# A four-layer decoder trunk: the instruction order drawn with the scheduler's time-line simulation

## The chip, the core and the metric

The kernel runs on one core of a Trainium2 chip. A core has TensorE (PE, matrix products; PEld is its weight load), VectorE (DVE), ScalarE (ACT), GpSimd (POOL) and SyncE (SP, which here issues the DMAs). Each engine takes its own instructions in order, and semaphores order them between engines. The metric is the device time of one execution in microseconds; less is better.

## The reference

The reference is a trunk of four pre-norm residual layers over 256 tokens of width 1024, in float32:

```python
for i in range(DEPTH):                       # 4 layers
    mixer = i % N_MIXERS                     # 0 attention, 1 convolution, 2 recurrence
    u = _rmsnorm(h, norm1_g[i])
    if mixer == 0:   h = h + _mla(u, ...)            # 16 heads, low-rank q and kv, rotary key
    elif mixer == 1: h = h + _conformer_conv(u, ...) # GLU, causal depthwise conv of 31 taps, LayerNorm, swish
    else:            h = h + _hgrn2(u, ...)          # gated linear recurrence, 8 heads of 128
    h = h + _swiglu(_rmsnorm(h, norm2_g[i]), ffn_w_gu[i], ffn_w_down[i])     # hidden width 2816
    gate = jax.nn.sigmoid(_rmsnorm(h, ple_norm_g[i]) @ ple_w_gate[i])
    h = h + (p[i] @ ple_w_proj[i]) * gate
return _rmsnorm(h, final_norm_g)
```

Layers 0 and 3 are attention, layer 1 the convolution, layer 2 the recurrence.

## The kernel before

The 256 tokens are two tiles of 128 rows (`t` = 0, 1). A product in float32 accuracy is made of three TensorE products of rounded parts: each operand x is split into a rounded `hi` and a remainder `lo`, and `mm` (L212) issues x_hi w_hi, x_hi w_lo and x_lo w_hi; all of them are recorded at L207, in the helper `matmul`. The transposed activations (`xT`, `aT`, `cT`, 128x128 blocks) stay in the array while the weights move, 512 columns at a time.

**Weights.** `granule` (L168) loads 128x1024 of a weight by DMA (`raw`, four buffers), lets ScalarE write `whi` (L180, or L185 with a norm's gain) and VectorE write `wlo` (L181, or L186 with the gain), in nine and eight buffers. Every weight thus costs about a microsecond of ScalarE and VectorE before TensorE can use it, and its buffer comes free when TensorE has read it.

**Activations.** `split_T` (L241) transposes four blocks into a PSUM bank named `tr` (L250; there are two such banks) and splits them (ScalarE L237, VectorE L238). `Norm.do` squares (L73), takes the reciprocal root by small steps on VectorE (L260 to L278, names rs_m, rs_h, rs_t, rs_y), and transposes h or, where the norm is applied ahead, hg (L82).

**The stages of a layer.** The attention makes q, k and v by groups of four heads (L619 to L631), then for two heads at a time the scores (L645 to L650), the softmax (maximum L653, exponent L659, reciprocal L664, scaling L666 on VectorE and L668 on ScalarE), the transposes of the probabilities `p` (L672 to L678), their copies `pT` (L675, L679) and the product with v (L682, L684). The out-projection and the part of the per-layer embedding (`embed`, from `pT` and `ple_w_proj`) are TensorE work that stands among these steps. The FFN (L345) runs over 11 column groups j: `up(j, t)` makes gate and up columns (tile mm), ScalarE the silu `sg` (L362), VectorE the product `ga` (L364), which is transposed for `down(j, t)`; the closure `turn` puts the transposes of one step into the products of the next, after two of its eight blocks (`mms`, argument `between`).

The recurrence (`hgrn`, L943 on) goes over four pairs of heads. `project` makes q, f, kb, v and g of a pair, 48 matmuls of 512 columns and 96 of 256. `recur` then works up eight levels of doubling block length; its core is

```python
ps = bank(); products(ps, q)                       # L995: kb x q, at = diagonal (L999), qf = q * f (L1004)
for l in range(8):
    if l < 4:
        ... nc.tensor.matmul(ps[:, hh, t], kb[:, hh, tok(t)], right(qf[:, hh, tok(t)]), ...)   # L1013
        V.copy_predicated(at..., self.pairs[:, l]..., ps...)                                    # L1014
    if l == 4: products(ps, qf)                                                                 # L995
    if l in (5, 6): ... matmuls on blocks of 32 and 64                                          # L1026
    if l == 6: V.copy_predicated(at..., self.union..., ps...)                                   # L1031
    if l < 7:
        V.tensor_tensor(out=blk(kb, 0), in0=blk(kb, 0), in1=wide(1), op=ALU.mult)               # L1040
        V.tensor_tensor(out=blk(qf, 1), in0=blk(qf, 1), in1=wide(0), op=ALU.mult)               # L1041
```

after which come a product kb x qf (L1050), the output products (L1056, L1058), their squares (L1059), a reciprocal root and the gated output `og` (L1065), which is transposed for the output projection. Each level reads what L1040 and L1041 of the level before wrote. While `recur` of one pair stands in the program, the weights and projections of the next pair stand behind it and are independent of it.

**What sets the order.** The program is written once, as a list of instructions with their dependences; the tile framework's scheduler then lays down one order for each engine, by running the list through a simulated machine and issuing, on each engine, what that machine finds ready, the earlier in the program first. A few rules in the kernel bind it (`issue_after` in `behind`, and `keep_in_program_order` for the matmuls of the convolution, `pinned`). Which buffer of a pool an allocation gets, and so which waits it carries, follows from the order too.

## Time and profile before

| | |
|---|---|
| median of 3 runs | 1402.45 us (1401.62 to 1406.26) |
| the profiled execution | 1401.64 us, its span 1399.9 us |
| TensorE busy | 1340.7 us, 96% of the span |
| VectorE, ScalarE busy | 920.0 us (66%), 789.0 us (56%) |
| DMA | 228.15 MB, mean 163 GB/s |
| granted TensorE clock, mean | 0.993 |

A row of a group names line, engine and operation, then the result, an arrow and the operands, then count, busy time, the mean duration of one in ns, and the idle time of the engine just before them with what ended it. A row of the waits names the waiting engine and line, what it waited for, the total in us, the number of waits and the longest. A row of a time line starts with the start and the length in us. A row of a stretch gives its length, then busy time and count of PE, PEld, DVE, ACT and POOL, the granted clock, the DMA share and GB/s. TensorE is shown by the profile with its instructions in passes, so that four matmuls of L1013 appear as eight.

The stretches, from the span's start: layer 0's attention to about 135 us, its FFN and gate to 345, the convolution (345 to 437), the FFN and gate of layer 1 to 690, the recurrence (690 to 860), the FFN and gate of layer 2 to 1065, layer 3's attention (1065 to 1175), its FFN and gate to the end.

### The profile page before, as it was taken

To read this page: it belongs to the slowest core of one execution; us is meant where nothing else is said; L and a number is where in the kernel's file an instruction comes from. 1 tells how busy PE (TensorE), PEld (TensorE's weight loads), DVE (VectorE), ACT (ScalarE), POOL (GpSimd) and SP (SyncE) were. 2 spreads that over 40 slices of the span, in tenths; PEclk is the share of its full clock that TensorE was granted. 3 is DMA by queue.
4 is the path that set the end of the run, shared out by engine and by line. 5 is a ranking of instruction groups with operands and counts; after the bars stand their busy time and mean duration, and the time that the engine had idled before them with its cause. 6 is when DMAs were issued, how large, how long until landed. Compare 5 with 4: busy or idle time off the path is not lost.

```text
span 1399.9 us, 20414 instructions
## 1 busy us (share of the span) xinstructions
PE 1340.7 (96%) x7153; PEld 1094.1 (78%) x7153; DVE 920.0 (66%) x1995; ACT 789.0 (56%) x1493; POOL 15.6 (1%) x51
## 2 busy tenths in 40 slices
PE   7889999999898999999999999999999999999997
PEld 6757878887886788888788887878878767788885
DVE  6774555548786855556887768555567776555556
ACT  6684545546625754455675546555556776554543
POOL 0000000000000000000000000000000000000000
PEclk9999999999999999999999999999999999999998
DMA  7242655555674666554474435655553433666632
GB/s 217 94 140 87 210 181 181 181 180 167 187 226 153 187 196 190 181 181 142 132 223 125 140 91 166 195 181 181 181 171 111 136 121 108 207 192 190 187 126 76
DMA packets 174023, 228.15 MB, mean 163 GB/s; under 512 B 11712, under 2 KB 138848, under 8 KB 173920
## 3 DMA queue, kind: packets, MB, share of 16 engines
q1 hardware_dynamic: 173920, 226.85, 52.1%
q8 instruction: 56, 0.92, 0.3%
q14 instruction: 47, 0.39, 0.1%
HBM read 222.27 MB, written 1.05 MB: 160 GB/s over the span
## 4 chain that ended last, share of the span: by engine, by line
PE 76%; DVE 8%; DMA 7%; ACT 6%; issue 3%; SPq 0%; DVEq 0%; ACTq 0%
PE mm L207 41%; PE acc L207 26%; PE tr L250 3%; DVE wlo L186 3%; DMA raw<-in_ffn_w_down_dram 2%; DMA raw<-in_ple_w_gate_dram 1%; PE acc L1013 1%; ACT whi L180 1%; ACT whi L185 1%; DMA raw<-in_mla_w_out_dram 1%; ACT p L659 1%; DVE wlo L181 1%; PE acc L649 1%; DMA raw<-in_ffn_w_gu_dram 1%; DMA raw<-in_conv_w_pw_dram 1%
## 5 line engine op out<-in xcount | busy, mean ns | idle before, releaser
L207 PE MATMUL mm<-whi,xT 128*128 128x512 f32 x1632 | 546.8, 398 | 1.2 <-ACT xT L237 0.9
L185 ACT ACTIVATE whi<-raw,gT 128x512 fp32r<-128x512 f32 (+3 forms) x604 | 387.0, 701 | 133.4 <-PE acc L207 59.7
L186 DVE SCALAR_TENSOR_TENSOR wlo<-raw,gT,whi 128x512 fp32r<-128x512 f32 (+3 forms) x604 | 410.1, 728 | 52.0 <-PE acc L207 33.1
L207 PEld LDWEIGHTS mm<-whi,xT 128*128 128x128 f32 x1632 | 305.6, 188 | 63.5 <-ACT xT L237 1.4
L207 PE MATMUL mm<-wlo,xT 128*128 128x512 f32 x816 | 320.6, 393 | 1.1 <-DVE wlo L181 1.1
L207 PE MATMUL acc<-whi,aT 128*128 128x512 f32 x704 | 233.1, 392 | 1.7 <-DVE aT L238 1.7
L181 DVE TENSOR_TENSOR wlo<-raw,whi 128x1024 fp32r<-128x1024 f32 x120 | 146.7, 1224 | 75.3 <-ACT whi L180 75.0
L180 ACT ACTIVATE whi<-raw 128x1024 fp32r<-128x1024 f32 x120 | 126.0, 1059 | 95.3 <-DMA raw<-in_ffn_w_down_dram 58.2
L207 PEld LDWEIGHTS mm<-wlo,xT 128*128 128x128 f32 x816 | 153.6, 188 | 30.6 <-DVE wlo L181 1.4
L207 PE MATMUL acc<-whi,xT 128*128 128x512 f32 (+2 forms) x544 | 167.1, 382 | 6.2 <-ACT xT L237 6.2
L207 PEld LDWEIGHTS acc<-whi,aT 128*128 128x128 f32 x704 | 131.5, 188 | 35.3 <-DVE aT L238 4.1
L207 PE MATMUL acc<-wlo,aT 128*128 128x512 f32 x352 | 138.7, 394 | 0.0
L364 DVE SCALAR_TENSOR_TENSOR ga<-mm,rs_y,sg 128x256 f32<-128x256 f32 x88 | 42.4, 481 | 139.9 <-ACT sg L362 139.9
L207 PEld LDWEIGHTS acc<-whi,xT 128*128 128x128 f32 x544 | 100.5, 190 | 22.4 <-ACT xT L237 7.0
L362 ACT ACTIVATE sg<-mm,rs_y 128x256 f32<-128x256 f32 x88 | 41.0, 466 | 134.8 <-PE mm L207 134.7
L207 PE MATMUL acc<-wlo,xT 128*128 128x512 f32 (+2 forms) x272 | 101.9, 375 | 0.0
L207 PEld LDWEIGHTS acc<-wlo,aT 128*128 128x128 f32 x352 | 66.2, 188 | 13.0
L238 DVE TENSOR_TENSOR aT<-tr,aT 128x256 fp32r<-128x256 f32 x88 | 37.0, 421 | 55.3 <-ACT aT L237 55.3
L207 PEld LDWEIGHTS acc<-wlo,xT 128*128 128x128 f32 x272 | 51.7, 190 | 7.6
L207 PE MATMUL mm<-whi,cT 128*128 128x384 f32 (+1 forms) x160 | 51.4, 381 | 5.7 <-ACT q L619 4.7
L73 ACT ACTIVATE junk<-h 128x512 bf16<-128x512 f32 x48 | 30.0, 625 | 45.8 <-DVE h L339 25.0
L237 ACT ACTIVATE aT<-tr 128x256 fp32r<-128x256 f32 x88 | 32.7, 371 | 28.1 <-PE tr L250 28.0
(250 smaller groups left out, 1455.4 us busy)
## 6 DMA issues: line engine op xcount, KB each, us to landing
raw<-in_ffn_w_gu_dram SPq DMA_DIRECT2D x352, 256.0 KB, 4.4
raw<-in_ffn_w_down_dram SPq DMA_DIRECT2D x88, 512.0 KB, 4.3
raw<-in_ple_w_gate_dram SPq DMA_DIRECT2D x32, 512.0 KB, 4.7
raw<-in_hgrn_w_in_dram SPq DMA_DIRECT2D x64, 256.0 KB, 3.8
raw<-in_mla_w_out_dram SPq DMA_DIRECT2D x16, 512.0 KB, 4.4
raw<-in_conv_w_pw_dram SPq DMA_DIRECT2D x32, 256.0 KB, 4.8
raw<-in_mla_w_in_dram SPq DMA_DIRECT2D x16, 336.0 KB, 3.8
raw<-in_mla_w_uq_dram SPq DMA_DIRECT2D x12, 384.0 KB, 3.8
```

The lines of the kernel that those rows point to most:

```text
L73: square = nc.scalar.activation(T.tmp("junk", [P, 512], 1, BF16), h[:, s], AF.Square, accum_out=ss[:, c : c + 1])
L180: nc.scalar.activation(hi[:, :used], raw[:, :used], AF.Copy)
L181: nc.vector.tensor_tensor(out=lo[:, :used], in0=raw[:, :used], in1=hi[:, :used].bitcast(F32), op=ALU.subtract)
L185: nc.scalar.activation(hi[:, s], raw[:, s], AF.Copy, scale=g[k])
L186: nc.vector.scalar_tensor_tensor(out=lo[:, s], in0=raw[:, s], scalar=g[k], in1=hi[:, s].bitcast(F32), op0=ALU.mult, op1=ALU.subtract)
L207: ins = self.nc.tensor.matmul(*args, **kw)
L237: a = self.nc.scalar.activation(hi, src, AF.Copy)
L238: v = self.nc.vector.tensor_tensor(out=lo, in0=src, in1=hi.bitcast(F32), op=ALU.subtract)
L250: nc.tensor.transpose(pt[:, (i - k0) * P : (i - k0 + 1) * P], src[:, i * P : (i + 1) * P], self.ident)
L362: nc.scalar.activation(sg, ps[:, :256], AF.Silu, scale=r)
L364: nc.vector.scalar_tensor_tensor(out=ga, in0=ps[:, 256:], scalar=r, in1=sg, op0=ALU.mult, op1=ALU.mult)
L649: nc.tensor.matmul(s1[:, hh], qT[:HD, h, P:], kT[:HD, h], start=True, stop=False)
```

## The change

One argument of the framework's context is set. The scheduler then takes its simulated machine's times from its time-line simulation instead of its default machine:

```diff
-    with tile.TileContext(nc) as tc, ExitStack() as ctx:
+    with tile.TileContext(nc, schedule_with_timeline_sim=True) as tc, ExitStack() as ctx:
         Trunk(ctx, tc, a, out[0]).run()
```

The instructions stay the same in kind, operands and number: 6633 matmuls on TensorE, 1995 operations on VectorE, 1341 activations on ScalarE, 692 DMAs from SyncE. Only their order on each engine, the buffers they use and the semaphores they wait for differ. Of TensorE's rows 1540 stand where they stood, and the others move by 13 places on average and 158 at most; on VectorE the mean move is 4.5 places, on ScalarE 1.8, and SyncE's DMAs nearly all stay.

Three places. First the recurrence of layer 2 on TensorE. In the names the last number tells the tile: kb_6986 and qf_7188 are those of head pair 0, kb_7367 and qf_7579 those of pair 1, mm_7336 a projection of pair 1. Before, a part of pair 0's levels:

```order
L1013 MATMUL acc_7200<-qf_7188,kb_6986 128x64 x4
L207 MATMUL mm_7336<-wlo_7094,xT_6687 128x512
L207 MATMUL mm_7336<-whi_7093,xT_6688 128x512
L207 MATMUL mm_7336<-whi_7102,xT_6687 128x512
L207 MATMUL mm_7336<-wlo_7103,xT_6687 128x512
L207 MATMUL mm_7336<-whi_7102,xT_6688 128x512
L207 MATMUL mm_7336<-whi_7102,xT_6687 128x512
L1013 MATMUL acc_7210<-qf_7188,kb_6986 128x64 x4
L207 MATMUL mm_7336<-wlo_7103,xT_6687 128x512
L207 MATMUL mm_7336<-whi_7102,xT_6688 128x512
```

Now, from the end of pair 0 into pair 1, ahead of this 13 weight matmuls and behind it five more rows of the same kind (two L1013, one L995 and the transposes of og_7301 and og_7304):

```order
L1026 MATMUL acc_7230<-qf_7188,kb_6986 32x32 x8
L1026 MATMUL acc_7230<-qf_7188,kb_6986 64x64 x4
L1050 MATMUL acc_7258<-qf_7188,kb_6986 128x128 x2
L1056 MATMUL acc_7263<-v_6951,at_7181 128x128
L995 MATMUL acc_7573<-q_7365,kb_7367 128x128 x4
L1013 MATMUL acc_7581<-qf_7579,kb_7367 128x64 x4
L1056 MATMUL acc_7263<-v_6980,at_7181 128x128
L1058 MATMUL acc_7263<-v_6951,ax_7259 128x128
L1013 MATMUL acc_7591<-qf_7579,kb_7367 128x64 x4
L1056 MATMUL acc_7263<-v_6951,at_7181 128x128
L1056 MATMUL acc_7263<-v_6980,at_7181 128x128
L1058 MATMUL acc_7263<-v_6951,ax_7259 128x128
```

The levels of pair 0 stood among the weight matmuls of pair 1's projection with six to eight between two levels. Now four levels of pair 0 stand 29 to 41 rows apart, the projection of pair 1 is used up, and the end of pair 0 and most of pair 1 stand one behind another. Shorter bunches of this kind stand between pairs 1 and 2, between pairs 2 and 3, in pair 3, and at the end.

On VectorE, in the same place, the steps of pair 0 (names kb_6986, qf_7188) and the weights of the pairs behind. Before:

```order
L186 SCALAR_TENSOR_TENSOR wlo_7503<-raw_7504,gT,whi_7502 128x512 x2
L1040 TENSOR_TENSOR kb_6986<-kb_6986,tot_1518_7228 128x16x16
L1041 TENSOR_TENSOR qf_7188<-qf_7188,tot_1518_7228 128x16x16
L186 SCALAR_TENSOR_TENSOR wlo_7512<-raw_7513,gT,whi_7511 128x512
L1040 TENSOR_TENSOR kb_6986<-kb_6986,tot_1520_7237 128x8x32
L1041 TENSOR_TENSOR qf_7188<-qf_7188,tot_1520_7237 128x8x32
L186 SCALAR_TENSOR_TENSOR wlo_7512<-raw_7513,gT,whi_7511 128x512
```

Now:

```order
L186 SCALAR_TENSOR_TENSOR wlo_7876<-raw_7877,gT,whi_7875 128x512 x2
L186 SCALAR_TENSOR_TENSOR wlo_7885<-raw_7886,gT,whi_7884 128x512 x2
L1040 TENSOR_TENSOR kb_6986<-kb_6986,tot_1518_7228 128x16x16
L1041 TENSOR_TENSOR qf_7188<-qf_7188,tot_1518_7228 128x16x16
L186 SCALAR_TENSOR_TENSOR wlo_7894<-raw_7895,gT,whi_7893 128x512
L1044 TENSOR_TENSOR tot_1588_7619<-tot_1586_7609 128x32
L186 SCALAR_TENSOR_TENSOR wlo_7894<-raw_7895,gT,whi_7893 128x512
L186 SCALAR_TENSOR_TENSOR wlo_7903<-raw_7904,gT,whi_7902 128x512 x2
L1040 TENSOR_TENSOR kb_6986<-kb_6986,tot_1520_7237 128x8x32
L1041 TENSOR_TENSOR qf_7188<-qf_7188,tot_1520_7237 128x8x32
```

One or two weight pieces stood between two levels; now it is four, and they belong to pair 2 (wlo_7876 to wlo_7903), a pair later than before.

Second, the FFN of layer 0 on TensorE: tr_2184 is the transposes of ga_2163, a gated product of one column group, whose up product ends 12 rows (acc_1562 and acc_1563, a down step) ahead of the first mm_2177. Before:

```order
L207 MATMUL acc_1563<-whi_2075,aT_1988 128x512
L207 MATMUL mm_2177<-whi_2093,xT_1386 128x512
L207 MATMUL mm_2177<-wlo_2094,xT_1386 128x512
L207 MATMUL mm_2177<-whi_2093,xT_1387 128x512
L207 MATMUL mm_2177<-whi_2093,xT_1386 128x512
L207 MATMUL mm_2177<-wlo_2094,xT_1386 128x512
L207 MATMUL mm_2177<-whi_2093,xT_1387 128x512
L250 MATMUL tr_2184<-ident,ga_2163 128x128 x2
```

Now (17 matmuls of mm_2177 stand ahead of the 12 of the down step):

```order
L207 MATMUL acc_1563<-wlo_2070,aT_1987 128x512
L207 MATMUL acc_1563<-whi_2069,aT_1988 128x512
L207 MATMUL acc_1563<-whi_2075,aT_1987 128x512
L207 MATMUL acc_1563<-wlo_2076,aT_1987 128x512
L207 MATMUL acc_1563<-whi_2075,aT_1988 128x512
L250 MATMUL tr_2184<-ident,ga_2163 128x128 x2
L207 MATMUL mm_2177<-whi_2111,xT_1387 128x512
```

The transposes stood 18 matmuls behind the end of the product that feeds them, and stand 29 behind it now; the down step moved from ahead of the next up product to behind most of it.

Third, the last softmax steps of layer 0's attention on TensorE; mm_1334 and mm_1353 are the out-projection of token tile 0, tr_1131 and tr_1242 the transposes of two successive pairs of heads. Before:

```order
L678 MATMUL tr_1137<-ident,p_281_1117 128x128
L682 MATMUL acc_1060<-pT_284_1129,v_823 64x256 x2
L684 MATMUL acc_1060<-pT_285_1130,v_864 64x128 x2
L672 MATMUL tr_1242<-ident,p_325_1227 128x128 x2
L674 MATMUL tr_1242<-ident,p_326_1228 128x128 x2
L678 MATMUL tr_1248<-ident,p_326_1228 128x128 x2
L207 MATMUL mm_1334<-whi_1165,xT_488 128x512
```

Now:

```order
L678 MATMUL tr_1137<-ident,p_281_1117 128x128
L682 MATMUL acc_1060<-pT_284_1129,v_823 64x256 x2
L684 MATMUL acc_1060<-pT_285_1130,v_864 64x128 x2
L207 MATMUL mm_1334<-whi_1177,xT_488 128x512
L207 MATMUL mm_1334<-wlo_1178,xT_488 128x512
L207 MATMUL mm_1353<-whi_1201,xT_488 128x512
L207 MATMUL mm_1353<-wlo_1202,xT_488 128x512
L672 MATMUL tr_1242<-ident,p_325_1227 128x128 x2
```

The first 24 matmuls of the out-projection stood behind this place and now stand ahead of tr_1131, and the next four between the two pairs' steps; the weights whi_1177 and whi_1201 are wanted that much earlier.

## The prediction

> **What bounds the kernel now.** I read the page first, then TensorE's waits, then the stretches stage by stage, and last the time line of single places. From the page:
>
> ```profile
> span 1399.9 us, 20414 instructions
> PE 1340.7 (96%) x7153; PEld 1094.1 (78%) x7153; DVE 920.0 (66%) x1995; ACT 789.0 (56%) x1493; POOL 15.6 (1%) x51
> PE 76%; DVE 8%; DMA 7%; ACT 6%; issue 3%; SPq 0%; DVEq 0%; ACTq 0%
> ```
>
> TensorE (PE) is busy for 1340.7 of 1399.9 us and carries 76% of the chain that ended last. It takes its instructions in order, so the time is its work plus its waits: 59 us idle. A new order adds or removes no work; it can only change the waits. The stretches that matter (first number PE's busy time; PEclk is the granted clock):
>
> ```profile
> 35.00:75.00 40.00, 35.53 (x215) 29.37 (x215) 28.22 (x92) 25.64 (x62) 3.60 (x7) 0.96 0.26 83
> 75.00:135.00 60.00, 53.16 (x283) 39.96 (x282) 37.62 (x81) 39.26 (x94) 0.00 (x0) 0.94 0.39 121
> 690.00:860.00 170.00, 165.53 (x1102) 141.11 (x1101) 128.46 (x341) 98.55 (x230) 0.00 (x0) 1.00 0.46 137
> 1100.00:1175.00 75.00, 69.88 (x413) 52.66 (x414) 48.51 (x123) 52.32 (x134) 1.49 (x4) 1.00 0.27 86
> ```
>
> These are the attention of layer 0 (two rows), the recurrence of layer 2, and the attention of layer 3. Idle: 4.5 + 6.8, then only 4.5 in 170 us, then 5.1. The recurrence, a chain of small steps, hardly stalls PE now; there is little to win there and much to lose. What PE waits for (total, times, longest):
>
> ```profile
> PE tr L250 <- DVE hg L82: 7.0, 4, 4.1
> PE acc L207 <- ACT xT L237: 6.2, 2, 5.2
> PE tr L672 <- DVE p L666: 4.1, 2, 3.9
> PE tr L250 <- DVE ga L364: 3.9, 5, 0.9
> PE acc L682 <- ACT pT L675: 3.4, 4, 1.6
> PE acc L207 <- DVE aT L238: 1.7, 4, 0.5
> PE acc L995 <- ACT kb L983: 1.4, 1, 1.4
> PE mm L207 <- ACT xT L237: 0.9, 2, 0.7
> ```
>
> **The recurrence, the largest term.** How one level runs before (start, length):
>
> ```profile
> 722.80 1.11 PE L1013 MATMUL acc<-qf,kb 128*128 128x64 f32 x8
> ...
> 723.72 0.48 PE L207 MATMUL mm<-wlo,xT 128*128 128x512 f32 x1
> ...
> 723.95 0.74 DVE L1014 COPY_PREDICATED at<-pairs,acc 128x256 f32<-128x256 uint8 x1 [0.43 <-PE acc L1013]
> 724.03 0.63 PE L207 MATMUL mm<-whi,xT 128*128 128x512 f32 x2
> ...
> 724.48 0.46 DVE L1040 TENSOR_TENSOR kb<-kb,tot 128x256 f32<-128x256 f32 x1
> 724.50 0.39 PE L207 MATMUL mm<-wlo,xT 128*128 128x512 f32 x1
> ...
> 724.85 0.41 DVE L1041 TENSOR_TENSOR qf<-qf,tot 128x256 f32<-128x256 f32 x1
> ...
> 725.32 0.97 PEld L1013 LDWEIGHTS acc<-qf,kb 128*128 128x128 f32 x8 [0.41 <-DVE qf L1041]
> ```
>
> From level to level 2.52 us. PE issues the level's products in 0.92 (722.80 to 723.72), VectorE starts 0.23 later, needs 1.31 for its three steps, and PE goes on 0.06 after. A weight matmul behind another takes 0.23 to 0.24 (two from 724.03 to 724.50). Six to eight weight matmuls fill the other 1.60 us. In the new order, the places shown in the section on the change have no weight matmul between levels, so each such level costs 1.60 us of idle PE. Why: VectorE now splits weights (L186, L181) ahead of the level's steps. Its prices in this stretch, with two of ScalarE's for the edges (L73 is the page's row, over the whole span; mean ns after the comma):
>
> ```profile
> L186 DVE SCALAR_TENSOR_TENSOR wlo<-raw,gT,whi 128x512 fp32r<-128x512 f32 x48 | 34.5, 748 | 2.8 <-ACT whi L185 2.1 <-issue 0.7
> L73 ACT ACTIVATE junk<-h 128x512 bf16<-128x512 f32 x48 | 30.0, 625 | 45.8 <-DVE h L339 25.0
> L237 ACT ACTIVATE xT<-tr 128x512 fp32r<-128x512 f32 x6 | 3.5, 592 | 0.3 <-PE tr L250 0.3
> L238 DVE TENSOR_TENSOR xT<-tr,xT 128x512 fp32r<-128x512 f32 x6 | 4.0, 687 | 1.4 <-ACT xT L237 1.4
> L181 DVE TENSOR_TENSOR wlo<-raw,whi 128x1024 fp32r<-128x1024 f32 x3 | 3.7, 1222 | 0.0
> L1065 DVE SCALAR_TENSOR_TENSOR og<-acc,rs_y,g 128x128 f32<-128x128 f32 x16 | 4.5, 344 | 0.1
> L1031 DVE COPY_PREDICATED at<-union,acc 128x512 f32<-128x512 uint8 x4 | 3.0, 740 | 1.3 <-PE acc L1026 1.3
> L276 DVE TENSOR_TENSOR rs_t<-rs_t,rs_h 128x4 f32<-128x4 f32 x12 | 1.9, 161 | 0.3
> ```
>
> Place A, between head pairs 0 and 1 (the 17 rows from the first L1026 to the transposes of og). Between the two L1026 rows VectorE does four weight pieces (4 x 0.75) before the next L1040 and L1041 (0.85); 14 weight matmuls ahead (3.2 us) hide most: PE waits 1.2. The next step waits for L1031, L1040, L1041: 0.23 + 0.74 + 0.85, some 1.85. The levels of pair 1: 1.1 (some products of pair 0 lie between), 1.6, 1.8 (small rs steps of 0.16 queue between), 1.6; then the transposes behind two more rs steps and four og of 0.34, 0.3. Sum 9.5 us.
>
> Place B, pairs 1 to 2: behind level 0 VectorE has two L181 (2.4), four L186 (3.0) and four small steps (0.6) before it takes level 1; PE's 22 cover matmuls (5 us) run out first: 3.2, then one bare level 1.6, then og 0.3: 5.1. Place C, pairs 2 to 3: two bare levels 3.2 and og 0.6: 3.8. Place D, pair 3: L1026 twice and L1050 without cover: 1.1 + 1.9 = 3.0. Place E, the end: 13 rs steps (2.1), the first two og (0.7) and ScalarE's square ahead of them stand between the last product and the transposes, and the 36 output matmuls that were spread among these now come before: 3.5. A to E: 24.9. Removed: the 1.4 on kb (its consumer now stands 40 matmuls later) and 0.7 of small ones. Net +22.8. Bounds: +14 if all queued weight pieces are done in time and only bare levels and the tail are left (eight levels 12.8, tail 3.5, less 2.1); +32 if the pieces queued in A and B are themselves late by one more pair each.
>
> **The clock.** PE's clock fell to half three times before. Stretches on one grid of 3.41 us:
>
> ```profile
> 99.11:102.53 3.42, 0.87 (x8) 0.49 (x8) 2.87 (x4) 3.40 (x6) 0.00 (x0) 1.00 0.87 260
> 102.53:105.94 3.41, 1.15 (x6) 1.00 (x7) 2.06 (x5) 3.35 (x12) 0.00 (x0) 0.50 0.86 271
> 105.94:109.35 3.41, 3.41 (x16) 2.17 (x16) 0.42 (x1) 0.60 (x1) 0.00 (x0) 0.50 0.50 172
> 358.50:361.91 3.41, 0.31 (x3) 0.34 (x4) 3.04 (x14) 1.20 (x4) 0.00 (x0) 1.00 0.85 275
> 361.91:365.33 3.42, 3.27 (x15) 2.75 (x14) 2.14 (x4) 2.68 (x5) 2.36 (x1) 0.51 0.03 11
> 437.00:440.41 3.41, 1.60 (x7) 0.78 (x8) 2.15 (x4) 1.71 (x3) 0.00 (x0) 1.00 0.81 261
> ```
>
> A stretch with 1.15 us or less of PE work is followed by one at 0.50; after the one with 1.60 the clock stayed. Half a stretch at 0.50 is lost: 1.7 us. Bare levels fill 1.11 of 2.52 us, 1.5 in a stretch, between the two. Place A is five stretches long and E has one nearly empty: from 0 to six drops, 0 to +10 us; I take one and a bit, +2, since 1.5 is nearer 1.60. [...]
>
> **Attention.** In layer 0 the new order puts 24 out-projection matmuls ahead of, and four to eight between, the softmax steps where PE stood 3.9 and 1.6 us and then ran 4.6 us of work at half clock (1.15 + 3.41, so 2.3 lost): 7.8 to win. Against it: the weights for them are wanted 1 to 5 us earlier than now, and ScalarE and VectorE, 39.26 and 37.62 of 60 us busy, prepare them; and the tail's transposes come back to back (2 us, next part). I take -4, from -9 (all won) to +3 (weights late by as much as they are wanted earlier). Layer 3 has the same move without a clock drop to undo: +1, from -4 to +6.
>
> **FFN.** All five waits for ga go: the transposes stood 18 matmuls behind the product that feeds them and now stand 29 behind, 11 x 0.23 = 2.5 us more, where the longest wait is 0.9. -3.9, at worst 0.
>
> **Edges of the stages.** At five norms the transposes of one token tile now follow the other's without matmuls between; with two banks the third group waits for a split: 0.23 + 0.59 + 0.69 less its own 0.4 = 1.1 each, 1.3 more in two; the conv's end has two such places, some 2. Less the waits on aT and xT that go (2.6): 5.5 + 1.3 + 2 - 2.6 = +6, from 0 to +9. At the start ScalarE does the first xT before two squares (L73, 0.63 each, and a read-out behind each) that stood ahead of it, in the 5.2 us wait: -1.5, from -2 to 0. Before the conv, the second half of h comes two weight pieces earlier on VectorE, in the 4.1 us wait for hg: -1.5, and half of the drop's 1.6 behind it: -2.3, from -4 to 0.
>
> **Sum.** -1.5 - 4 - 2.3 - 3.9 + 6 + 22.8 + 2 + 1 = +20.1. The profiled execution took 1401.64 us (1.7 around the span), 0.8 under the median of 1402.45, so the forecast is 1422 us.
>
> **Rivals.** *Attention pays for it (faster).* The two attentions idle 4.5 + 6.8 + 5.1 = 16.4 us and lose about 4 by the clock. If the weights of the out-projections are there when PE asks, all but 2 can go, -18; with -3.9 in the FFN, -2 at the start, -4 before the conv, +6 at the edges and the recurrence at its lower bound, +14: -8, 1394 us. For it: the cover stands exactly at the long waits. Against it: it takes the best of five terms, and the transfer of these weights is already awaited at that place (DMA share 0.87 in the row from 99.11). It decides if the first out-projection matmuls of layer 0 start without a wait. 12%. *The recurrence lags more (slower still).* The clock halves in most stretches of A and in B and E, +8 over my 2, the queued pieces are late, +6, the attentions come out at zero instead of -3: 1402 + 20 + 17, 1439 us. For it: PE's share in the bare levels is close to the 1.15; against it: 1.60 kept the clock. 18%. *Nothing to see.* The instructions are the same, so gains and losses cancel: recurrence at +14, attention -9, edges 0: within 4 us of 1402. 8%. My forecast's own range, 1408 to 1433, has 62%.
>
> **The numbers.** A measurement of this kernel can tell about 0.3%, 4.2 us. Faster by more: the first rival, 0.12. Within: the third and the low edge of the forecast, 0.09. Slower: the rest, 0.79. The range for 8 in 10, 1400 to 1440, holds my case and the second rival's middle, and leaves out the faster end.
>
> **What would show it.** In the recurrence, waits of PE's L1013, L1026 and L1050 on qf and kb of 20 to 25 us in all, where they were under 1 (right), or under 10 (wrong: VectorE kept up). PE's idle in that stage should go from 4.5 to about 27 us. The waits tr <- ga should be gone, and tr L672 <- p with them; if in their place stand waits of mm L207 on wlo or whi of w_out, attention gave nothing. Clock rows at 0.50 near 103 should vanish, and may appear in the recurrence. The forecast is wrong as a whole if PE's idle there stays under 12 us.

## The result, and the profile after

The changed kernel took **1480.82 us** (1476.94 to 1483.56, 4 runs) against 1402.25 us of the kernel before in the same comparison: a ratio of **1.055** (95% interval 1.0532 to 1.057), 78 us slower. The forecast was 1422 us with a range of 1400 to 1440. The sign was right and the size was a quarter of what came. The profiled execution of the change is the fastest of its four, at 1476.94 us.

The page of the changed kernel, with the same three lines that were shown of before:

```profile
span 1475.1 us, 20459 instructions
PE 1368.8 (93%) x7153; PEld 1121.5 (76%) x7153; DVE 930.1 (63%) x1995; ACT 795.0 (54%) x1493; POOL 12.9 (1%) x51
PE 54%; DVE 7%; ACT 3%; DMA 2%; issue 1%; SPq 0%; DVEq 0%; POOL 0%; ACTq 0%; POOLq 0%
```

The two PE numbers split the loss. The span grew by 75.2 us. TensorE runs the same 7153 rows, yet it is busy for 28.1 us more (1340.7 to 1368.8): that is work done at a lower clock, as the granted clock shows (0.968 on average, 0.993 before). In the change's trace a weight matmul of 512 columns starts 0.43 us after the one ahead of it where the clock is 0.50, and 0.23 where it is 1.00 (medians). The other 47.1 us are idle time (59.2 to 106.3). The stretches of the first attention, the recurrence and the second attention, from the same steps of the program as those shown before:

```profile
35.00:75.00 40.00, 34.70 (x199) 27.77 (x197) 27.21 (x89) 23.06 (x61) 1.83 (x6) 0.96 0.22 73
75.00:140.80 65.80, 58.90 (x318) 45.51 (x317) 34.11 (x72) 36.79 (x92) 0.29 (x1) 0.95 0.28 89
715.80:916.60 200.80, 173.78 (x1093) 152.87 (x1092) 128.54 (x343) 98.43 (x230) 0.00 (x0) 0.91 0.38 113
1160.80:1247.20 86.40, 77.57 (x440) 59.30 (x440) 48.40 (x119) 49.10 (x131) 1.54 (x5) 0.96 0.22 72
```

The recurrence takes 200.8 us where it took 170. Its idle is 27.0 us (200.80 less 173.78), where the prediction said "from 4.5 to about 27". But its clock is 0.91 where it was 1.00, and PE's busy time there is 8.3 us longer (165.53 to 173.78). What PE waits for now, in chosen rows:

```profile
PE tr L250 <- DVE hg L82: 13.3, 2, 7.8
PE acc L682 <- ACT pT L675: 6.1, 4, 2.7
PE tr L250 <- DVE xT L238: 5.9, 7, 1.1
PE mm L207 <- ACT cT L237: 5.6, 2, 2.8
PE acc L1013 <- DVE rs_t L276: 4.7, 3, 2.1
PE tr L250 <- DVE og L1065: 3.3, 1, 3.3
PE acc L1050 <- DVE qf L1041: 3.1, 2, 1.5
PE acc L1013 <- DVE rs_t L275: 2.9, 2, 1.6
PE acc L1026 <- DVE qf L1041: 2.6, 2, 1.7
PE acc L207 <- ACT whi L180: 2.0, 1, 2.0
PE tr L250 <- DVE ga L364: 1.4, 1, 1.4
PE acc L995 <- DVE rs_t L276: 1.3, 1, 1.3
```

Two kinds are new and two have grown. New are the recurrence's bunches, the five rows of L1013, L1026, L1050 and L995 with the one on og, 17.9 us, and the waits for cT in the attentions. Grown are the attentions' waits for pT (3.4 before) and those for hg at the head of a layer: 7.0 us in four waits before, now two, one before the conv (7.8) and one before the recurrence (5.5). The wait of tr L672 on p, 4.1 us before, is gone, of five waits for ga (3.9) one is left (1.4), and those for q (L619) fell from 4.7 to 1.0.

The time by stages, each ended by its last TensorE instruction. Waits are PE's gaps of over 0.1 us. "Half clock" is half of PE's busy time in stretches with a granted clock near 0.5. The convolution is counted here with its output projection, to 471 us before; the list of stretches ahead of the prediction ends it at 437. Over the whole span the two add up to the loss within 2 us:

| stage | length before, after | change | waits before, after | half clock before, after |
|---|---|---|---|---|
| attention, layer 0 | 135.0, 140.8 | +5.8 | 16.3, 20.5 | 4.4, 5.1 |
| its FFN and gate | 215.2, 219.6 | +4.4 | 2.2, 3.7 | 0, 0 |
| convolution | 121.2, 131.6 | +10.4 | 8.3, 16.5 | 1.8, 6.1 |
| FFN and gate, layer 1 | 220.6, 225.7 | +5.1 | 1.4, 4.6 | 0, 1.7 |
| recurrence | 160.8, 191.6 | +30.8 | 4.2, 25.6 | 0, 14.6 |
| FFN and gate, layer 2 | 214.5, 218.7 | +4.2 | 1.4, 3.2 | 0, 1.6 |
| attention, layer 3 | 107.6, 119.1 | +11.5 | 7.1, 12.6 | 0, 6.3 |
| FFN and gate, layer 3 | 215.0, 217.9 | +2.9 | 2.7, 4.5 | 0, 0 |

No stage gained. Waits rise by 47.6 us in all, the loss at half clock by 29.2. Stage by stage they do not add up as well: in the recurrence the two give 36.0 us for a loss of 30.8, and in each FFN less than the loss. PE's busy time in the recurrence's stretch rose by 8.3 us, so the 14.6 there is an upper figure.

### The profile page after: what moved, and what is told of

It reads as the page before. It is cut to its first block, busy times and chain, and to the rows that moved or that the text cites. A ratio compares the mean times of both kernels' runs of the same rounds, so it can differ in the third digit from the quotient of the medians.

```text
span 1475.1 us, 20459 instructions
## 1 busy us (share of the span) xinstructions
PE 1368.8 (93%) x7153; PEld 1121.5 (76%) x7153; DVE 930.1 (63%) x1995; ACT 795.0 (54%) x1493; POOL 12.9 (1%) x51
## 4 chain that ended last, share of the span: by engine, by line
PE 54%; DVE 7%; ACT 3%; DMA 2%; issue 1%; SPq 0%; DVEq 0%; POOL 0%; ACTq 0%; POOLq 0%
PE mm L207 31%; PE acc L207 17%; DVE wlo L186 2%; PE tr L250 2%; PE acc L1013 1%; DMA raw<-in_ple_w_gate_dram 1%; DMA raw<-in_hgrn_w_in_dram 1%; DVE h L339 1%; DMA raw<-in_ffn_w_gu_dram 1%; PE acc L995 1%; ACT whi L185 1%; PE tr L631 1%; DVE xT L238 0%; ACT p L659 0%; ACT junk L73 0%
## 5 line engine op out<-in xcount | busy, mean ns | idle before, releaser
L207 PE MATMUL mm<-whi,xT 128*128 128x512 f32 x1632 | 525.4, 399 | 6.3 <-ACT xT L237 4.0
L185 ACT ACTIVATE whi<-raw,gT 128x512 fp32r<-128x512 f32 (+3 forms) x604 | 388.4, 701 | 131.6 <-PE mm L207 46.9
L180 ACT ACTIVATE whi<-raw 128x1024 fp32r<-128x1024 f32 x120 | 126.0, 1058 | 75.6 <-DMA raw<-in_ffn_w_down_dram 47.5
L207 PEld LDWEIGHTS acc<-whi,aT 128*128 128x128 f32 x704 | 132.2, 188 | 30.8 <-ACT aT L237 1.7
L207 PE MATMUL acc<-wlo,xT 128*128 128x512 f32 (+2 forms) x272 | 105.4, 389 | 2.1 <-DVE wlo L186 2.1
L207 PE MATMUL mm<-whi,cT 128*128 128x384 f32 (+1 forms) x160 | 54.5, 397 | 9.8 <-ACT cT L237 5.6
```

The lines of the kernel that those rows point to most:

```text
L180: nc.scalar.activation(hi[:, :used], raw[:, :used], AF.Copy)
L185: nc.scalar.activation(hi[:, s], raw[:, s], AF.Copy, scale=g[k])
L207: ins = self.nc.tensor.matmul(*args, **kw)
```

## The experiments

The instructions of both kernels are the same, so a part of one order can be put into the other. After the program is written, a table of instruction numbers chains instructions of one engine by an order-only edge; the scheduler must then issue those in the table's order and places the others as it would. The edit is the same in all but the fillers and the FFN's line, and only the table differs:

```diff
+def follow(tc):
...
+    for steps in table.values():
...
+                tc.add_manual_dep(
+                    traced[name], before,
+                    mybir.DependencyInfo(mybir.DependencyClass.NoSync, mybir.DependencyReason.DATA), reason="follow",
+                )
...
         Trunk(ctx, tc, a, out[0]).run()
+        follow(tc)
```

**The recurrence put back, and the recurrence alone.** The first kernel is the change with the recurrence's instructions chained as they stood before on all engines; the second is the kernel before with these instructions chained as the change has them.

> The changed kernel, with the instructions of the recurrence stage (layer 2, from its projections to the end of its residual) held on every engine in the order that they had before; all else is drawn by the time-line simulation as in the change. In the traces this stage grew by 30.8 us. Theory A (the loss lies where the order differs, stage by stage): that comes back, 1450 us (1445 to 1455), and the stages in front and behind keep their times. Rival B (the stage only shows what earlier stages delay, through buffers, transfers or the phase of the clock): less than half comes back, above 1465 us.

> The kernel before, with the recurrence stage alone held in the order of the changed kernel. Theory A: 1402 + 31 = 1433 us (1428 to 1438). Rival B: under 1417 us. My prediction's price for this stage, 25 us, gives 1427.

Measured: 1450.62 us (ratio 1.0342, 1.032 to 1.0364) and 1430.66 us (1.0197, 1.0177 to 1.0217). Putting the recurrence back wins 30 us, its order alone costs 28. The waits of the second kernel, with the rest of the program in the old order:

```profile
PE acc L1013 <- DVE rs_t L276: 4.7, 3, 2.1
PE tr L250 <- DVE og L1065: 3.3, 1, 3.3
PE acc L1050 <- DVE qf L1041: 3.1, 2, 1.5
PE acc L1013 <- DVE rs_t L275: 2.9, 2, 1.6
PE acc L1026 <- DVE qf L1041: 2.6, 2, 1.7
PE acc L995 <- DVE rs_t L276: 1.3, 1, 1.3
```

They are, row for row, those of the change. The bunches stall in the old surroundings as in the new.

**Which engine's order it is.** The change, with only VectorE and ScalarE of the recurrence chained as before, and with only TensorE chained as before.

> The changed kernel, with the recurrence's instructions on VectorE and ScalarE alone held in the order of before; TensorE is left to the time-line simulation, which still sets the levels some 31 weight matmuls apart and then runs out of them. Theory P (TensorE's order costs the time): little comes back, 1470 to 1485 us, with waits of TensorE on qf as in the change. Rival V (my prediction: VectorE's weight pieces ahead of the level's steps cost it): most of the 31 us comes back, under 1460 us.

> The changed kernel, with the recurrence's matmuls on TensorE alone held in the order of before (six to eight weight matmuls between two levels); VectorE and ScalarE are drawn by the time-line simulation. Theory P: nearly all of the 31 us comes back, 1448 to 1457 us. Rival V: TensorE stands at each level behind VectorE's weight pieces, above 1465 us.

Measured: 1503.17 us (2 runs, span 1503.5) and 1464.87 us (2 runs, span 1463.8). Neither theory gets its number: old VectorE and ScalarE orders with TensorE left to the time-line simulation are worse than the change by 22 us, and the old TensorE order under the new ones wins 16 of the 30. The longest waits of the first:

```profile
PE mm L207 <- ACT f L982: 7.4, 4, 2.9
PE acc L1026 <- DVE qf L1041: 6.9, 8, 0.9
PE acc L1050 <- DVE qf L1041: 6.6, 4, 2.0
```

All four pairs now stall at L1026 and L1050. The trace of this run shows why: in pairs 0 to 2 most of the first levels stand 21 to 35 weight matmuls apart on TensorE, and in all four pairs none stands between the two L1026 steps and L1050, so the cover is used up at the end of each pair. The projections' waits for ScalarE's f, 7.4 us, are 0.3 in the change. With TensorE's order put back, the longest wait of the stage's own steps is one of 4.6 us (`acc L995 <- ACT kb L983`). So TensorE's order alone is worth about half of the stage's loss. The prediction's cause, weight pieces in VectorE's order, gets no support from the first run, since VectorE's and ScalarE's old order alone did not help. That the orders fit each other only as a set is argued from these two runs.

**The clock.** If the halved clock is a cost of its own, TensorE must win by being kept busy with useless work during the same waits. `fill` issues matmuls whose result nobody reads (the identity with the causal mask, 256 columns, bfloat16) into the bank that the next real product or transpose then overwrites from its start; they stand right ahead of that instruction. 232 of them go before the longest waits of the change and all real instructions are chained in the change's order:

```diff
+    def fill(self, ps, n):
+        for _ in range(n):
+            ins = self.nc.tensor.matmul(ps[:, :S], self.ident_bf, self.causal.rearrange("p h n -> p (h n)"), start=True, stop=True)
...
+                fence = T.split_T(hg, self.x, 0, t, 60 if t == NT - 1 else 0)
...
+            self.T.fence = self.T.split_T(self.hg, self.x, 0, NT - 1, 44)
...
+                    if gi == 0 and t == 0:
+                        self.fill(pq, 22)
...
+                        if (hp, l) in ((1, 1), (1, 2), (1, 3), (2, 2), (2, 3), (3, 2), (3, 3)):
+                            self.fill(ps, 6)
...
+                        self.split_T(*out.pop(0), fill=24 if last_og and len(out) == 1 else 0)
```

> The changed kernel, its whole order held on every engine, with 232 small matmuls more on TensorE (128x256, bf16, 0.12 us each) that write a bank which the next real instruction overwrites. They stand right ahead of long waits: before the transposes of hg at the head of the convolution (60) and of the recurrence (44), before the first products with cT in both attentions (22 each), before the levels of the bunches in the recurrence (6 each at ten places) and before the last transposes of og (24). In the change TensorE runs at half clock for 86 us in 15 spells and loses 35 us by it; nine of these spells (60 us) follow the waits that are filled. Theory C (the half clock is a cost of its own): the filled waits keep the clock, some 24 us come back less a few for fillers that overrun, 1461 us (1453 to 1468). Rival D (the chains of small steps set the time, and a faster TensorE only waits longer): 1476 to 1486 us.

Measured: 1465.4 us (1464.2 to 1473.47), ratio 1.0459 (1.043 to 1.0488): 15.4 us less than the change by the medians and some 13 by the ratios, with every real instruction in the same order. A spell is an unbroken time at half clock. Leaving out the one at the program's end, time at half clock falls from 88.7 us in 15 spells to 51.2 us in 10, and the matmuls' loss from about 35 to about 23 us. The profiled execution is the one at 1473 us, 8 above the median, so its trace may show less than the median gained. The granted clock agrees in every execution: 0.981 to 0.989 with the fillers, 0.965 to 0.969 in the change. Theory C holds: the half clock is a cost of its own, and about half of its 28 us can be had back without touching the order. The same on the kernel before, its own order chained, ahead of its three waits on hg (4.1), p (3.9) and q (2.3), 81 matmuls in all:

```diff
+                fence = T.split_T(hg, self.x, 0, t, 32 if t == NT - 1 else 0)
...
+                    if i == 0 and gi == 0 and h0 == 0:
+                        self.fill(s0, 19)
...
+                    if i == 0 and gi == 3 and h0 == 0:
+                        self.fill(t0, 30)
```

> The kernel before, its whole order held, with fillers ahead of the three waits that its half-clock spells follow: 19 before the first scores of layer 0, 30 before the transposes of its seventh softmax, 32 before hg at the head of the convolution. Before, the three spells cost 6.0 us. Theory C: 1397 us (1395.5 to 1399.5). Rival D: 1401 to 1404 us.

Measured: 1398.57 us (1395.69 to 1400.02, 12 runs), ratio 0.9968 (0.9957 to 0.998). The kernel before gets faster by a third of a per cent from work that nobody needs. Theory C holds here too: the granted clock was 0.994 to 0.996 in all 12 executions, against 0.986 to 0.992 in the 23 of the kernel before beside them. No run chained the order without fillers, so it is the clock that ties the gain to them. Two spells are left, one of them at the conv's end (436 us), where the profile of before had none.

**The FFN's transposes, and the stages without chains.** The prediction's FFN term said that later transposes of ga would win 3.9 us. The first kernel does only this, in the kernel before: they come four weight tiles behind instead of two. The second is the change with both attentions, the convolution and the recurrence chained as before, so that FFN, gates and the start keep the new order. The third is the reverse for the attentions: before, with only the two attentions chained as the change has them.

```diff
-            if k == 2 and between is not None:
+            if k == 4 and between is not None:
```

> The kernel before (default order), where the FFN's transposes of ga go into the next product after four of its eight blocks and not after two, so that they stand 24 matmuls behind the product that feeds them (18 before, 29 in the change). The FFN term of my prediction: the five waits for ga, 3.9 us, go and nothing takes their place: 1398.5 us (1397 to 1400). Rival: the down step then waits for aT, or the order drawn around it is worse: 1401 to 1406 us.

> The changed kernel, with both attentions, the convolution and the recurrence held in the order of before on every engine, so that only the FFNs, the gates and their edges are in the new order. In the traces these grew by 4.5, 5.1, 4.1 and 2.9 us. Theory A (the loss lies stage by stage): 1402 + 17 = 1419 us (1413 to 1425). Rival B: under 1409 us, if these edges only show what the neighbours delay.

> The kernel before, with only the two attention layers held in the change's drawn order on all engines. Theory A (each stage loses what its own order costs, my two attention terms of -4 and +1 were wrong by themselves): the stages lengthen as in the change, by 5.8 us and 11.5 us, so 1402.3 + 17.3 = 1419.5 us (1416 to 1423). Theory B (their loss came from the state of the clock that the other stages' waits left behind): 1400 to 1411 us.

Measured: 1401.0 us (ratio 0.9986, 0.9973 to 1.0), 1421.9 us (1.0137, 1.0106 to 1.0167) and 1426.25 us (1.0164, 1.0137 to 1.019). In the first, no wait on ga is left, but what it wins cannot be told from nothing. The second lies 19 us above the kernel before, near the 17 of these stages' rows in the table. That agreement is in part chance: in its trace the convolution, held in the order of before, loses 7.5 us at half clock, where it lost 1.8 before. The third lies 3 us above what theory A allowed. The attentions' stages lengthen by 5.0 and 10.6 us, as expected; the other 8 us lie in stages whose order is that of before. The clock spells moved: seven in this run (41.0 us), among them at 367, 446, 705 and 729 us, where the shown run of before has one of 3.4 us between 350 and 850. So theory A holds for the stages themselves, and the total carries a part that came with the moved spells; what moved them was not shown. In per cent the three parts are 1.97 (recurrence), 1.64 (attentions), 1.37 (FFN, gates, start), together 4.98 of 5.51. The rest, some 7 us, is left for the convolution, whose stage lost 10.4; no run had its order alone, and the parts carry clock losses of other stages, so this split is rough.

**The head of the convolution.** Its two rival causes: TensorE's order, or the steps of the norm that stand in line behind weight pieces on ScalarE and VectorE. The change, with VectorE and ScalarE of the first gate and the convolution chained as before, and with TensorE alone chained there.

> The change, with VectorE and ScalarE of the first gate and the conv layer held in the order of the kernel before; TensorE keeps its drawn order. Theory P (the long wait for hg at the head of the conv layer, 7.8 us for 4.1, comes from TensorE's order, which takes the gate's matmuls that had stood behind the third block's transposes ahead of them, so that too little is left to cover the last block's chain): next to nothing is won, 1477 to 1484 us. Theory V (the chain's own steps stand behind weight pieces that wait for their transfers on ScalarE and VectorE): the stage falls from 131.6 to some 122 us, total 1468 to 1474 us.

> The change, with TensorE alone of the first gate and the conv layer held in the order of the kernel before; VectorE and ScalarE keep theirs. Theory P: the third block's transposes come ahead of some 26 matmuls of the gate again, the waits for weights and hg there fall from 2.1 + 7.8 to about 4.1 us, and the half-clock stretch behind them goes too: the stage falls from 131.6 to 121 to 124 us, total 1470 to 1475 us. Theory V: 1477 to 1484 us.

Measured: 1483.54 us (1.0555, 1.0522 to 1.0588) and 1475.33 us (1.0513, 1.0495 to 1.053). The first changes nothing; the second wins 5.5 us, just outside what was expected of it. The time lines show the block of transposes of hg ahead of the last and the last (start, length, wait). The change:

```profile
359.63 1.04 PE L250 MATMUL tr<-ident,hg 128*128 128x128 f32 x8
...
377.11 1.94 PE L250 MATMUL tr<-ident,hg 128*128 128x128 f32 x8 [7.76 <-DVE hg L82]
```

Before:

```profile
343.78 1.06 PE L250 MATMUL tr<-ident,hg 128*128 128x128 f32 x8 [0.55 <-DVE hg L82]
...
361.60 1.61 PE L250 MATMUL tr<-ident,hg 128*128 128x128 f32 x8 [4.13 <-DVE hg L82]
```

TensorE's old order in the change:

```profile
353.31 1.06 PE L250 MATMUL tr<-ident,hg 128*128 128x128 f32 x8 [0.55 <-DVE hg L82]
...
372.77 1.94 PE L250 MATMUL tr<-ident,hg 128*128 128x128 f32 x8 [4.21 <-DVE hg L82]
```

VectorE's and ScalarE's old order in the change:

```profile
361.62 1.04 PE L250 MATMUL tr<-ident,hg 128*128 128x128 f32 x8
...
379.50 1.82 PE L250 MATMUL tr<-ident,hg 128*128 128x128 f32 x8 [4.62 <-DVE hg L82]
```

From one block's transposes to the last's there are 17.8 us before, 17.5 in the change, and 17.9 with VectorE and ScalarE put back: their order does not set it. TensorE's order sets how much work stands inside. Before, 25 of the gate's matmuls with xT came behind the first of the two blocks; the change takes all but one of them ahead of it, so the cover runs out at 369 us, and 2.05 (for whi L180) and 7.76 us are waited. The 4.62 of the last of these is no gain: the same few matmuls took longer there, 6.8 of the 17.9 us being at half clock. With TensorE's order back the long wait is 4.21, but the interval grows to 19.5 us and a wait of 1.3 appears in it; of the 14.8 us that the first FFN, its gate and the convolution lost together, 5.4 come back. Theory P holds for the place, and what keeps the other 9 us of these stages was not taken apart further.

**Both gains on the kernel before.**

```diff
-            if k == 2 and between is not None:
+            if k == 4 and between is not None:
...
+                fence = T.split_T(hg, self.x, 0, t, 32 if t == NT - 1 else 0)
...
+                        self.fill(s0, 19)
...
+                        self.fill(t0, 30)
```

> The kernel before with both edits at once: the filler matmuls ahead of its three longest waits (by themselves 0.9968 of the kernel before) and the FFN's late transposes two weight tiles later (by themselves 0.9986, not told apart from no change). Theory A (the two gains lie in different stages and add up): 1402.5 * 0.9968 * 0.9986 = 1396.1 us (1393.5 to 1398.5), ratio some 0.9955. Theory B (the second edit won nothing): 1398.5 us, ratio 0.9968.

Measured: 1396.61 us (1393.89 to 1400.29, 12 runs), ratio 0.9961 (0.9945 to 0.9977). It beats both kernels, by 0.4% the one before. Its interval holds 0.9968 too, so whether the second edit adds anything stays open.

## Why the prediction was right in sign and wrong in size

**The recurrence (+22.8): the places right, the price high, the cause not shown.** Idle PE in that stretch went from 4.5 to 27.0 us, but 3.7 of the 22.5 are the wait for hg at its head (1.8 to 5.5), which stood in no term, so that the hit on "about 27" is partly luck. The places themselves cost some 18 to 19, inside the bounds of 14 to 32. The sign that the prediction had set, 20 to 25 us of waits at L1013, L1026 and L1050, came out at 14.3, of which the profile books 6.7 to qf and 7.6 to the rs_t steps that stand behind qf's in VectorE's order. They stalled where they were named: behind pair 0, PE waited 1.70, 1.55, 0.99 and 1.35 us at these rows of the change, for prices of 1.1 to 1.85:

```profile
785.18 0.68 PE L1026 MATMUL acc<-qf,kb 128*64 128x64 f32 x8 [1.70 <-DVE qf L1041]
787.41 0.68 PE L1050 MATMUL acc<-qf,kb 128*128 128x128 f32 x4 [1.55 <-DVE qf L1041]
791.53 1.08 PE L1013 MATMUL acc<-qf,kb 128*128 128x64 f32 x8 [0.99 <-DVE qf L1041]
...
796.52 1.94 PE L1013 MATMUL acc<-qf,kb 128*128 128x64 f32 x8 [1.35 <-DVE rs_t L276]
```

Place E, priced at 3.5, took 3.3 (og). A bare level took 1.28 to 1.6 us at most places, where 1.60 was the price. That the order of the stage makes these waits is shown twice over: the same rows appear in the old surroundings, and the stage gets back all but about 5 us when its order goes back. The reason that the prediction gave, weight pieces ahead of the level's steps on VectorE, holds in the trace at the first waits of places A and B only (three pieces stand ahead of A's L1040 at 784.37); in C and D no piece stands there. In a bare level TensorE and VectorE take turns, and VectorE is idle as well:

```profile
796.52 1.94 PE L1013 MATMUL acc<-qf,kb 128*128 128x64 f32 x8 [1.35 <-DVE rs_t L276]
...
798.50 0.42 DVE L1014 COPY_PREDICATED at<-pairs,acc 128x256 f32<-128x256 uint8 x1 [1.07 <-PE acc L1013]
...
799.17 0.42 DVE L1041 TENSOR_TENSOR qf<-qf,tot 128x256 f32<-128x256 f32 x1
...
799.74 2.04 PE L995 MATMUL acc<-qf,kb 128*128 128x128 f32 x8 [1.28 <-DVE rs_t L276]
```

**The clock (+2): this step failed, and is the largest miss, about half of the whole.** It measured +28.1 us by PE's busy time and +29.2 by the stretches; the rest of the miss are waits of the attentions, the convolution and the FFNs, below. The prediction began with "it can only change the waits", and that does not hold here: the same matmuls were busy for 28.1 us more. The argument was that a bunch fills 1.5 us of a stretch of 3.41 and that 1.60 had kept the clock. Two things were wrong with it. The stretches were emptier than the mean of 1.5, and fuller ones halved too:

```profile
867.59:871.00 3.41, 1.82 (x18) 1.72 (x16) 2.48 (x13) 0.37 (x2) 0.00 (x0) 0.99 0.00 0
871.00:874.41 3.41, 2.13 (x11) 1.97 (x11) 2.76 (x11) 0.00 (x0) 0.00 (x0) 0.50 0.00 0
874.41:877.83 3.42, 3.37 (x12) 2.59 (x12) 1.76 (x5) 0.77 (x2) 0.00 (x0) 0.51 0.00 0
...
830.04:833.45 3.41, 1.32 (x13) 1.21 (x11) 3.31 (x12) 1.81 (x4) 0.00 (x0) 0.99 0.88 311
833.45:836.87 3.42, 2.14 (x11) 1.99 (x10) 2.55 (x12) 0.14 (x1) 0.00 (x0) 0.50 0.56 192
...
785.67:789.08 3.41, 1.86 (x19) 1.75 (x17) 1.53 (x4) 0.64 (x3) 0.00 (x0) 1.00 0.83 229
789.08:792.49 3.41, 2.42 (x23) 2.26 (x21) 2.00 (x4) 0.37 (x2) 0.00 (x0) 1.00 0.02 5
```

With 1.82 and 1.32 us of work the next stretch is at half clock; with 1.86 it is not. And a stretch at half clock that still stands in a bunch (2.13, 2.14) is followed by another at half; nine of the change's 15 spells last two stretches (6.8 us). The term also looked at the recurrence alone. Up to half of the new loss, 14.6 us by the table and 8.3 by PE's busy time, is in that stage; for new drops in layer 3's attention (6.3), the conv (4.3) and elsewhere (4) the prediction had no term.

**Attention (-4 and +1): wrong sign.** The waits rose by 4.2 and 5.5 us, and layer 3 lost 6 us more by the clock. As predicted, the 3.9 us wait on p is gone, and in layer 0 its spell of 6.8 us near 103 with it (two of 3.4 us, near 93 and 117, come in its place). But the 24 out-projection matmuls that fill it are not new cover; they and the other independent matmuls are taken from elsewhere. One softmax step of layer 3, the change and then the same step before:

```profile
1199.86 0.64 PE L631 MATMUL tr<-ident,q 128*96 128x128 f32 x4 [0.52 <-DVE pT L679]
1203.17 1.12 PE L682 MATMUL acc<-pT,v 128*64 128x256 f32 x4 [2.67 <-ACT pT L675]
```

```profile
1118.20 0.65 PE L682 MATMUL acc<-pT,v 128*64 128x256 f32 x4 [0.58 <-ACT pT L675]
```

The transposes of cg, ahead of the first products with cT, are another. Before, 3.4 us of products with xT stood between the first token tile's transposes and the first product with cT in layer 0, and no wait for cT is in the list. In the change only a masking matmul stands there, and PE waits 2.85 us; in layer 3 it waits 2.74 behind the last two transposes of the second tile (5.6 together in the row above). The prediction had read only the places where a wait of before would go, not those that lose their cover.

**Before the conv (-2.3): wrong sign.** The steps on VectorE were taken as what ends the wait; the interval between the two blocks stayed at 17.5 to 17.9 us with either order of them, and TensorE's cover inside it decides. Waits of the conv stage rose by 8.2 us.

**FFN (-3.9) and edges (+6): near in waits, short in all.** Of the ga waits 2.5 us went. The back-to-back transposes are there as described, seven waits of tr on xT, 5.9 us, up to 1.1 each as priced. FFN and gates still lose 16.6 us in all by the table: 8.3 are waits, among them new ones on pieces of weights (whi and wlo, up to 1.1 us), 3.3 the clock; the rest was not traced to a cause.

**The start (-1.5): right.** The wait of the first products on xT fell from 5.2 to 3.4 us.

Of the rivals, "the recurrence lags more" came closest (1439), at 18%. Its argument of the clock was right; its late pieces did not come, and the attentions, which it had at zero, lost 17.3 us. The result lies above all that was forecast.

## What to carry to other kernels

When an order is drawn anew, do not only price the waits that it removes: independent work is a fixed stock, and each piece that is moved ahead of one wait is missing behind another; list for each chain step what stood between it and the step before, in both orders. Bunched stalls were followed here by TensorE's granted clock at 0.50 (behind stretches of 3.41 us with 1.32 and 1.82 us of work, for example), which by estimate loses up to half of each such stretch, 1.7 us; in this kernel a stall cost about 1.6 times its length on the whole (75 us lost for 47 of waits). Where a wait cannot be removed, useless matmuls in it may pay: they won 0.3% here.

## What the runs showed of the hardware

In the traces of before and of the change the granted clock is 1.00 or 0.50. Their 18 half-clock spells ahead of the program's end last 3.4, 6.8 or 10.2 us and, in each trace, start whole multiples of 3.41 us apart; that is the grid of the rows here. On it, over both traces, from 20 us on and without the program's end: a stretch at full clock with 1.45 us or less of PE work was always followed by one at half clock (14 of 14: 0.12 to 1.45). Between 1.64 and 2.18 us it went either way (four halved, at 1.82, 1.93, 1.98 and 2.18; seventeen not). Above 2.18 none halved. A stretch at half clock with 2.83 us of work or less was followed by another (12 of 12), and with 2.97 or more the clock came back (18 of 18). What decides between 1.64 and 2.18 is not shown; PE's busy time is modelled in part. These bounds belong to the two traces and are no rule. In the other twelve a stretch with 1.55 us kept its clock (the run with the recurrence's order alone, at 36 us), one with 2.5 halved (TensorE's order back in the recurrence, at 1166 us), and three stretches at half clock that were busy throughout were still followed by another at half clock. One of them, in the run with both gains:

```profile
436.72:440.13 3.41, 3.41 (x11) 2.30 (x11) 0.49 (x2) 1.47 (x2) 0.00 (x0) 0.50 0.73 263
440.13:443.55 3.42, 3.42 (x9) 2.65 (x10) 2.94 (x20) 0.60 (x1) 0.00 (x0) 0.50 0.01 2
443.55:446.96 3.41, 3.41 (x20) 2.83 (x19) 1.25 (x5) 1.13 (x2) 0.00 (x0) 1.00 0.00 0
```

The spells differ from one execution to the next, and from order to order: the mean granted clock of the kernel before ran from 0.986 to 0.993 over its executions, its trace showed 3 spells (at 38, 103 and 362 us), and with only the FFN's transposes moved it showed five, at 39, 104, 360, 438 and 698 us. That this comes from where a wait falls on the grid is the author's estimate and was not shown. A part of any small gain or loss of this kernel may be that. Why the time-line simulation spaces the recurrence's levels as it does, which of its prices differs from the chip, was not tried and stays open.
